# Turning values, keys and outputs by crossbar transfers and GpSimd copies in place of TensorE, from the eighth segment on

## The chip, the cores and the metric

The kernel runs on one core of a Trainium2 chip. A core has a matrix engine (TensorE, rows "PE" for its matmuls and "PEld" for its weight loads), three engines for elementwise work (VectorE "DVE", ScalarE "ACT", GpSimd "POOL"), SyncE ("SP"), which here only starts transfers, and 16 DMA engines that carry them. Each engine works through its own instructions in order and stops at an instruction whose semaphores have not come. The metric is device time in microseconds of one launch. The kernel before takes 2149.38 us, the median of three runs (2148.78 to 2149.49).

## What is computed

One layer of a backbone over 2048 latent tokens of width 1024, with 256 context tokens in front of it. One projection feeds two groups of heads: eight heads of a gated linear recurrence, run forward and backward, and a short convolution. Their outputs go through one output projection. Around the change stands the recurrence:

```
S_t = diag(f_t) S_{t-1} + k_t v_t^T        o_t = S_t^T q_t       (forward and backward, o_f + flip(o_b))
k   = 1 - f          f = lb + (1 - lb) * sigmoid(z)
y   = o * rsqrt(mean(o*o, over the head) + EPS) * onorm_w * silu(gate)
```

Per head k, v, q and o have 128 channels; all of it is float32.

## The kernel before

**Tiling.** The tokens are cut into four groups of 512. A segment is one head on one group: 8 heads x 4 groups = 32 segments. Even heads go through their groups forwards, odd ones backwards. A tile of a segment has channels on the 128 partitions and 512 tokens along the row; its four chunks have 128 tokens each.

**Windows.** The program is written window by window. A window holds the projection of one segment as two or three `units` (one for both gates, one for value and query, in every second window one more for the output gates), and beside them the `chain`, which is the recurrence of the segment before, and `extra` steps: the second direction of the head before, its normalisation and its outputs. A unit consists of seven products (function `seven`, lines 930 to 932) of 12 matmuls each, in a scheme that saves the eighth product of a 2x2 block multiplication. Each step of chain and extra has a weight (`paced(weight, fn)`, table PACE); `merge_steps` lays the steps over the window in proportion to their weights, and `tick`, called after every three matmuls of a product, writes the next step when its share has been reached. So weights decide where among the products' matmuls a step stands in TensorE's order. After the 32 segments come four windows of the convolution, 14 of paired groups, and the output projection.

**The chain of a segment** (`scan_steps`): `value_turn` turns the value tile by four TensorE transposes into PSUM, copied out by ScalarE (lines 555 and 557); five `levels` and `level6` build the in-segment attention from small matmuls on K and Q, while VectorE multiplies K and Q by running products of f (L485, L492); the last matmuls of that are L657, and the last change of K stands behind them. `key_turn` then turns both halves of K, one per direction, into PSUM (L672, eight transposes), ScalarE copies them out (L674); `states` multiplies turned keys with turned values (L681, four matmuls per direction, two instructions each in the profile) and updates the states; `outp` makes the output (L737, L738). For the outputs, `y_steps` scales the output tile (L825), turns it (`turn`, L831), and VectorE multiplies the turned tile, read from PSUM, by the gate (L833).

**Queues.** All loads and stores but 15 of the last stores stand in SP's order. Among them are `hop` loads (L1389): nine buffers of 512 KB hold the operands of the projection, and each load waits until TensorE has read the buffer's old content. Transfers use eight semaphores in turn, so a transfer also waits for the one eight places ahead of it. GpSimd copies Q aside for every second level (`held`, L608) and puts diagonal blocks into the attention tile (L665).

Tiles tagged `pair` are four buffers of 2 KB per partition, used before the change by the operand stores of the early windows and by the scan of the output weights in the last heads.

## Time and profile before

| | |
|---|---|
| median of three runs | 2149.38 us |
| span of the profiled execution | 2150.1 us |
| granted TensorE clock | 0.994 of full speed |
| PE matmuls busy | 2073.2 us, 96% |
| VectorE, ScalarE, GpSimd busy | 77%, 55%, 9% |
| share of the DMA engines' time, main queue | 42.9% |
| first and last turned key tile of a segment | 126.0 to 1265.3 us |

The profiled execution's own time is its span of 2150.1 us, 0.7 us above the median of the runs. A busy TensorE is the union of matmuls whose ends are modelled; the spacing of the starts of successive matmuls says more about what one costs. Rows of groups name line, engine, operation, tiles, shape and count, then busy time, the mean length of one, and idle time before it with what ended it. A number behind "us to landing" counts from the issue to the arrival of the whole transfer.

### The profile page before, as it was taken

What the parts mean: (1) busy time and instruction counts of PE and PEld (TensorE: products, weight loads), DVE (VectorE), ACT (ScalarE), POOL (GpSimd) and SP (SyncE); (2) the same over time, 40 slices, a digit from 0 to 9 for tenths busy, and PEclk for the clock granted to TensorE, in tenths of its full rate; (3) what the DMA queues carried; (4) which work ended last, traced back from release to release, by engine and by line L of the source; (5) the groups of instructions that cost most, each with busy time, mean ns of one, the idle gap of its engine ahead of it and who ended that gap; (6) DMA issues with size and microseconds to landing.
All of it is one profiled execution on the core that took longest, in us unless ns stands there. A gap on an engine that the chain in (4) does not pass through costs nothing.

```text
span 2150.1 us, 53050 instructions
## 1 busy us (share of the span) xinstructions
PE 2073.2 (96%) x22111; PEld 1466.0 (68%) x22111; DVE 1645.8 (77%) x3413; ACT 1192.2 (55%) x2406; POOL 191.8 (9%) x272
## 2 busy tenths in 40 slices
PE   5988999999999999999999999999999999999998
PEld 2877878888888888888888887444444444444443
DVE  6787988878778787788687887678778656687775
ACT  7965666757567666576676654354445423333332
POOL 0121111111111110111110100000000000000000
PEclk9999999999999999999999999999999999999999
DMA  9567533442344233424543458933442105642421
GB/s 356 191 207 265 178 126 134 137 158 72 114 129 146 97 114 109 153 81 142 194 131 127 130 165 260 285 108 110 134 149 93 54 23 196 206 143 92 137 79 59
DMA packets 185798, 311.02 MB, mean 145 GB/s; under 512 B 13010, under 2 KB 114770, under 8 KB 183764
## 3 DMA queue, kind: packets, MB, share of 16 engines
q1 hardware_dynamic: 183396, 303.68, 42.9%
q8 instruction: 173, 2.83, 0.5%
q10 hardware_dynamic: 2160, 3.93, 0.5%
q14 instruction: 69, 0.57, 0.1%
HBM read 240.19 MB, written 67.37 MB: 143 GB/s over the span
## 4 chain that ended last, share of the span: by engine, by line
PE 65%; DVE 18%; ACT 7%; DMA 4%; issue 3%; POOL 1%; SPq 0%; POOLq 0%; ACTq 0%; DVEq 0%
PE sa L930 8%; PE sa L932 8%; PE sa L931 8%; PE sb L930 4%; PE sb L932 4%; PE sb L931 4%; PE sa_o L930 2%; PE sa_o L931 2%; PE sa_o L932 2%; DVE Q L492 2%; PE sc L930 2%; PE sc L931 2%; PE sc L932 2%; DVE K L485 2%; PE T L681 2%
## 5 line engine op out<-in xcount | busy, mean ns | idle before, releaser
L931 PEld LDWEIGHTS <-e_p 128*128 128x128 f16 x1332 | 130.4, 98 | 59.8 <-issue 10.3
L930 PEld LDWEIGHTS <-e_p 128*128 128x128 f16 x1332 | 130.4, 98 | 54.0 <-issue 1.1
L601 ACT ACTIVATE km<-K 128x512 f32<-128x512 f32 x192 | 129.6, 675 | 67.2 <-DVE K L485 61.1
L932 PEld LDWEIGHTS <-e_p 128*128 128x128 f16 x1332 | 130.3, 98 | 51.4
L485 DVE TENSOR_TENSOR K<-K,tot 128x512 f32<-128x512 f32 x192 | 132.2, 689 | 42.9 <-ACT km L601 25.3
L492 DVE TENSOR_TENSOR Q<-Q,tot 128x512 f32<-128x512 f32 x192 | 132.5, 690 | 34.9 <-POOL qm L608 19.5
L608 POOL COPY qm<-Q 128x512 f32<-128x512 f32 x96 | 80.8, 842 | 794.4 <-DVE Q L492 778.7
L931 PEld LDWEIGHTS <-whib_p 128*128 128x128 f16 x888 | 86.9, 98 | 42.1 <-issue 8.8
L930 PEld LDWEIGHTS <-whib_p 128*128 128x128 f16 x888 | 86.8, 98 | 36.7 <-issue 0.8
L930 PEld LDWEIGHTS <-whia_p 128*128 128x128 f16 x888 | 87.0, 98 | 35.7 <-DMA hop3B<-Hd3B 2.3
L932 PEld LDWEIGHTS <-wloa_p 128*128 128x128 f16 x888 | 87.0, 98 | 34.2
L931 PEld LDWEIGHTS <-whia_p 128*128 128x128 f16 x888 | 87.0, 98 | 33.9 <-issue 1.5
L932 PEld LDWEIGHTS <-wlob_p 128*128 128x128 f16 x888 | 86.8, 98 | 34.0
L157 ACT ACTIVATE e_p<-ws_p,sc_p 128x512 f16<-128x512 f32 x108 | 77.5, 718 | 54.9 <-DVE ws_p L444 42.0
L665 POOL COPY A<-Ac 32x128 f32<-32x128 f32 x128 | 77.2, 603 | 128.3 <-ACT A L661 110.6
L853 ACT ACTIVATE cv<-c,small 128x512 f32<-128x512 f32 (+1 forms) x36 | 24.2, 673 | 106.8 <-DVE c L871 61.1
L937 ACT ACTIVATE u<-sa,sx_w 128x256 f32<-128x256 f32 (+1 forms) x111 | 58.1, 524 | 43.5 <-PE sa L932 34.7
L937 ACT ACTIVATE p<-sa,sx_w 128x256 f32<-128x256 f32 (+1 forms) x111 | 57.4, 517 | 39.9 <-PE sa L932 39.8
L158 DVE SCALAR_TENSOR_TENSOR e_p<-ws_p,sc_p,e_p 128x512 f16<-128x512 f32 x108 | 79.4, 750 | 0.0
L409 ACT ACTIVATE junk<-ws_p 128x1024 f16<-128x1024 f32 x72 | 75.7, 1052 | 6.5 <-DMA ws_p<-in_w_in 6.3
L1596 POOL TENSOR_TENSOR x_o<-x_o,fw 128x512 f32<-128x512 f32 x1 | 1.3, 1262 | 868.0 <-ACT junk L1587 868.0
L937 ACT ACTIVATE p<-sb,sx_w 128x256 f32<-128x256 f32 (+1 forms) x111 | 57.8, 521 | 30.8 <-PE sb L932 28.0
(858 smaller groups left out, 7036.3 us busy)
## 6 DMA issues: line engine op xcount, KB each, us to landing
ws_p<-in_w_in SPq DMA_DIRECT2D x72, 512.0 KB, 4.3
y_o<-yT SPq DMA_DIRECT2D x32, 512.0 KB, 4.3
xt_x<-in_x SPq DMA_DIRECT2D x16, 512.0 KB, 6.2
wa<-in_w_ada SPq DMA_DIRECT2D x16, 512.0 KB, 10.2
Gd<-zs SPq DMA_DIRECT2D x32, 256.0 KB, 2.7
sg<-Gd SPq DMA_DIRECT2D x32, 256.0 KB, 4.4
wos<-in_w_out SPq DMA_DIRECT2D x32, 256.0 KB, 5.0
yT<-y SPq DMA_DIRECT2D x32, 256.0 KB, 2.9
```

The source lines that it names most:

```text
L157: S.activation(hi, src, AF.Copy, scale=st[:, 0:1])
L158: V.scalar_tensor_tensor(lo, src, st[:, 0:1], hi, ALU.mult, ALU.subtract)
L409: S.activation(junk.rearrange("p (k n) -> p k n", k=KT), stage[i], AF.Abs, accum_out=r)
L485: V.tensor_tensor(m, m, sub(cur, nb + 1, [[2, np_], [-(nb + 1), 2], [0, B]]), ALU.mult)
L492: V.tensor_tensor(m, m, sub(cur, 1, [[2, np_], [nb - 1, 2], [0, B]]), ALU.mult)
L601: S.activation(sub(s.km, 0, [[2 * B, n // (2 * B)], [B, 2], [1, B]]), mix(s.K, n, B, n // (2 * B)), AF.Copy)
L608: G.tensor_copy(sub(qm, 0, [[2 * B, n // (2 * B)], [B, 2], [1, B]]), mix(s.qf, n, B, n // (2 * B)))
L665: G.tensor_copy(A3[js, :, js], s.Ac[js])
L930: PE.matmul(ps, hi[:, k], rh, start=start and k == 0, stop=False, skip_group_check=not start)
L931: PE.matmul(ps, hi[:, k], right(name, 1, k), start=False, stop=False, skip_group_check=not start)
L932: PE.matmul(ps, lo[:, k], rh, start=False, stop=k == nk - 1, skip_group_check=not start)
L937: last_keep.append(S.activation(r, ps, AF.Copy, scale=sx))
```

## The change

For the 25 segments from the eighth on (head 1's last segment, all of heads 2 to 7), three turns leave TensorE: values, both directions' keys, and outputs (the last not for head 7). A turn becomes three steps (`turn_steps`): `over` sends the tile, read as 128 x 1024 halves of 16 bits, through the DMA crossbar, which puts columns on partitions; `back` gathers the halves of each number with four plain transfers inside SBUF, each of 64 partitions x 4 x 128 halves; `join` lets GpSimd write the two planes of halves interleaved into a ring tile. All transfers are issued by SP, the buffers are of tag `pair`. A turn thus adds one crossbar transfer, four plain ones and one copy; there are 96 turns. Output tiles are multiplied by the gate from SBUF instead of PSUM (`product`). Value turns start ahead of `begin` and end ahead of the third level; the key steps have weights that add to 4.2 where `key_turn` had 1.0.

```diff
+BY_DMA = 7
...
+    def turn_steps(src, make, nm, after=(1.0, 1.0)):
+
+        t = {}
+
+        def over():
+            t["a"] = hp.tile([P, 2 * NCH, P], U16, tag="pair", name=f"ta_{nm}", bufs=4)
+            SY.dma_start_transpose(t["a"], src().bitcast(U16))
+
+        def back():
+            t["b"] = hp.tile([P, NCH, 2, P], U16, tag="pair", name=f"tb_{nm}", bufs=4)
+            for h in range(2):
+                for b in range(2):
+                    SY.dma_start(t["b"][64 * b:64 * b + 64, :, h, :], t["a"][h::2, b::2, :])
+
+        def join():
+            G.tensor_copy(make().bitcast(U16).rearrange("p (c d h) -> p c d h", c=NCH, h=2),
+                          t["b"].rearrange("p c h d -> p c d h"))
+
+        return [paced(after[0], over), paced(after[1], back), paced(0.3, join)]
...
-        return ([paced("values", s.value_turn), paced("begin", s.begin_levels)]
-                + [paced("levels", lambda: s.levels(0)), paced("held", lambda: s.held(1)),
-                   paced("levels", lambda: s.levels(2)), paced("held", lambda: s.held(3)),
+        values = [paced("values", s.value_turn)]
+        held_v = []
+        if s.fast:
+            values, held_v = [], turn_steps(lambda: s.vT, new_value, f"v{s.nm}", (0.2, 0.2))
+        keys = [paced("keys", s.key_turn)]
+        if s.fast:
+            s.kT = []
...
+            two = [turn_steps(lambda i=i: s.K[:, i * s.n:(i + 1) * s.n], lambda i=i: new_keys(i), f"k{s.nm}{i}") for i in range(2)]
+            keys = ([paced(0.0, two[0][0][1]), paced(1.2, two[1][0][1]), paced(0.0, two[0][1][1]), paced(1.2, two[1][1][1]),
+                     paced(0.2, two[0][2][1]), paced(1.6, two[1][2][1])])
+        return (values + held_v[:1] + [paced("begin", s.begin_levels)] + held_v[1:2]
+                + [paced("levels", lambda: s.levels(0)), paced("held", lambda: s.held(1))]
+                + held_v[2:] + [paced("levels", lambda: s.levels(2)), paced("held", lambda: s.held(3)),
                    paced("levels", lambda: s.levels(4))]
-                + [paced("held", lambda: s.held(5)), paced("level6", s.level6), paced("keys", s.key_turn), paced("states", states),
+                + [paced("held", lambda: s.held(5)), paced("level6", s.level6)] + keys + [paced("states", states),
                    paced("out", outp)])
...
+        def product():
+            y = ring(f"y_{s.nm}")
+            V.scalar_tensor_tensor(y, s.oT, onw, s.sg, ALU.mult, ALU.mult)
+            put_y(h.hd, s.tok0 // GW, y)
+
+        end = [paced("turn_y", turn)]
+        if s.fast and h.hd < HEADS - 1:
+            end = turn_steps(lambda: s.o, make, f"o{s.nm}", (0.5, 0.5)) + [paced("turn_y", product)]
...
             s = Seg(hd, g * GW, GW, 0, f"{hd}_{g}")
+            s.fast = hd * NG + i >= BY_DMA
```

How the change moves instructions is seen best at the second segment of head 4, whose chain stands in a window with two units.

SP's order in that window before, from the first operand load of the next segment but one to the load that follows the output (hop: operands, zs and sg: output gates, y: an output tile):

```order
L1389 DMA hop19T_12048<-Hd3T_100 128x2048
L753 DMA yT_113<-y_0_12066 128x512
L818 DMA sg_2_12592<-Gd_108 128x512
L1389 DMA hop19B_12137<-Hd3B_101 128x2048
L1389 DMA hop19T_12153<-Hd3B_99 128x2048
L1389 DMA hop19B_12204<-Hd3B_101 128x2048
```

and now (ta: turned halves, tb: gathered halves; o, k and v name the turn):

```order
L120 DMA_TRANSPOSE ta_o_0_12035<-Q_0_10371 128x8x128
L1444 DMA hop19T_12137<-Hd3T_100 128x2048
L126 DMA tb_o_0_12142<-ta_o_0_12035 64x4x128 x4
L120 DMA_TRANSPOSE ta_k_10_12211<-K_1_11165 128x8x128
L120 DMA_TRANSPOSE ta_k_11_12213<-K_1_11165 128x8x128
L1444 DMA hop19B_12223<-Hd3B_101 128x2048
L126 DMA tb_k_10_12230<-ta_k_10_12211 64x4x128 x4
L126 DMA tb_k_11_12235<-ta_k_11_12213 64x4x128 x4
L1444 DMA hop19T_12249<-Hd3B_99 128x2048
L1444 DMA hop19B_12274<-Hd3B_101 128x2048
L795 DMA yT_113<-y_0_12264 128x512
```

The two crossbar transfers of the keys and their eight plain transfers stand between operand loads; one such load stands between `over` and `back`, and two stand behind the eight.

TensorE's order at the same segment, before, from the key turn to the products of turned keys and values (sc: an accumulator of the projection):

```order
L672 MATMUL kT_10_12161<-ident,K_1_11091 128x128 x4
L672 MATMUL kT_11_12168<-ident,K_1_11091 128x128 x4
...
L932 MATMUL sc_12157<-hop18B_11634,wloa_p_10426 128x256
L681 MATMUL T_10_12184<-v_1_11818,kT_10_12166 128x128 x4
L681 MATMUL T_11_12197<-v_1_11818,kT_11_12173 128x128 x4
```

and now, from the last attention matmuls:

```order
L680 MATMUL A_4_1_12147<-Q_1_11695,K_1_11165 32x64 x16
...
L985 MATMUL sb_12204<-hop18B_11771,e_p_10493 128x256
L986 LDWEIGHTS e_p_10493
L986 MATMUL sb_12204<-hop18B_11771,e_p_10493 128x256
L704 MATMUL T_10_12283<-v_1_11981,kT_10_12257 128x128 x4
L704 MATMUL T_11_12296<-v_1_11981,kT_11_12259 128x128 x4
```

The eight transposes are gone, and between the last attention matmuls and the first product of keys and values now stand 69 matmuls of 128 x 256; before there were 36 and the eight transposes.

GpSimd's order there, before and now:

```order
L608 COPY qm_4_1_12053<-Q_1_11615 128x512
L665 COPY A_1_12112<-Ac_1_11871 32x4x32 x4
L608 COPY qm_4_2_12387<-Q_2_12277 128x512
```

```order
L688 COPY A_1_12183<-Ac_1_11948 32x4x32 x4
L129 COPY oT_0_12221<-tb_o_0_12142 128x1024
L129 COPY kT_10_12257<-tb_k_10_12230 128x1024
L129 COPY kT_11_12259<-tb_k_11_12235 128x1024
L631 COPY qm_4_2_12466<-Q_2_12367 128x512
```

Copies of an output tile and of both key tiles now stand between the diagonal blocks of this segment and the first copy of Q of the next.

More of the change, by code (lines that the diff above doesn't have):

```diff
@@ L13 @@
 I32 = mybir.dt.int32
+U16 = mybir.dt.uint16
 U8 = mybir.dt.uint8
@@ L512, in __init__ @@
             s.small = n < GW
+            s.fast = False
             s.f = s.K = None
@@ L740, in outp, with new_value, new_keys @@
             S.activation(s.o, po, AF.Copy)
-        return ([paced("values", s.value_turn), paced("begin", s.begin_levels)]
-                + [paced("levels", lambda: s.levels(0)), paced("held", lambda: s.held(1)),
-                   paced("levels", lambda: s.levels(2)), paced("held", lambda: s.held(3)),
+        def new_value():
+            s.v = ring(f"v_{s.nm}")
+            return s.v
+        values = [paced("values", s.value_turn)]
[5 more added lines that the diff above has]
+            s.kT = []
+            def new_keys(i):
+                s.kT.append(ring(f"kT_{s.nm}{i}"))
+                return s.kT[i]
+            two = [turn_steps(lambda i=i: s.K[:, i * s.n:(i + 1) * s.n], lambda i=i: new_keys(i), f"k{s.nm}{i}") for i in range(2)]
[4 more added lines that the diff above has]
+                + held_v[2:] + [paced("levels", lambda: s.levels(2)), paced("held", lambda: s.held(3)),
                    paced("levels", lambda: s.levels(4))]
-                + [paced("held", lambda: s.held(5)), paced("level6", s.level6), paced("keys", s.key_turn), paced("states", states),
+                + [paced("held", lambda: s.held(5)), paced("level6", s.level6)] + keys + [paced("states", states),
                    paced("out", outp)])
@@ L834, in turn, with make @@
             put_y(h.hd, s.tok0 // GW, y)
-        return ([paced(0.0, gate)] if own_gate else []) + [paced("scale", scale), paced("turn_y", turn)]
+        def make():
+            s.oT = ring(f"oT_{s.nm}")
+            return s.oT
+        def product():
[5 more added lines that the diff above has]
+            end = turn_steps(lambda: s.o, make, f"o{s.nm}", (0.5, 0.5)) + [paced("turn_y", product)]
+        return ([paced(0.0, gate)] if own_gate else []) + [paced("scale", scale)] + end
     class Conv:
```

## The prediction

> **What bounds the kernel now.** I read the busy times by stretch first, over the stretch in which segments 8 to 32 run their chains:
>
> ```profile
> core 0: us, PE busy (x) PEld busy (x) DVE busy (x) ACT busy (x) POOL busy (x), PEclk, DMA share, GB/s
> 400.00:700.00 300.00, 295.37 (x4446) 261.59 (x4444) 241.04 (x532) 191.38 (x427) 40.09 (x56) 1.00 0.38 123
> 700.00:1000.00 300.00, 295.76 (x4449) 261.94 (x4447) 239.12 (x537) 194.37 (x444) 39.62 (x56) 1.00 0.37 119
> 1000.00:1270.00 270.00, 261.14 (x4134) 231.15 (x4133) 210.72 (x461) 179.61 (x424) 37.66 (x56) 0.99 0.43 139
> ```
>
> TensorE is busy for 852 of 870 us; VectorE has 20% to spare, ScalarE 35%, GpSimd 87%, the DMA engines 60%. The waits of TensorE in that stretch are small:
>
> ```profile
> PE A L631 <- POOL qm L608: 6.1, 7, 2.7
> PE sa L930 <- ACT u L937: 3.0, 10, 0.6
> PE A L631 <- DVE Q L492: 1.9, 7, 0.3
> PE sa L930 <- DVE f L941: 1.7, 5, 0.5
> PE T L681 <- ACT kT L674: 1.6, 3, 0.8
> ```
>
> So each matmul taken away shortens the span by its own length, and each new wait of TensorE lengthens it: the two sides of the sum are counted on this one engine.
>
> **What goes.** 25 segments lose 4 value and 8 key transposes, 21 lose 4 output transposes: 300 + 84 = 384. One costs what it pushes the next weight load back. Loads of the projection follow every 0.11 us; with four transposes between two of them the gap is 0.54:
>
> ```profile
> 705.81 0.10 PEld L932 LDWEIGHTS <-e_p 128*128 128x128 f16 x1
> 705.92 0.47 PEld L672 LDWEIGHTS kT_c<-ident,K_c 128*128 128x128 f32 x4
> 706.35 0.10 PEld L930 LDWEIGHTS <-e_p 128*128 128x128 f16 x1
> ```
>
> Four cost 0.43 us, one 0.108, 384 cost 41.5 us. The busy times of the groups give the upper bound:
>
> ```profile
> L672 PE MATMUL kT<-ident,K 128*128 128x128 f32 x256 | 34.3, 274 | 1.0 <-DVE Q L777 1.0
> L831 PE MATMUL oT<-ident,Q 128*128 128x128 f32 x128 | 20.1, 277 | 0.7 <-ACT Q L825 0.5
> L555 PE MATMUL vt<-ident,vT 128*128 128x128 f32 x128 | 19.8, 278 | 0.4 <-DVE s_c L704 0.4
> ```
>
> 200 x 34.3/256 + 84 x 20.1/128 + 100 x 19.8/128 = 55.5 us, but that counts tails of matmuls under which the next one runs. I take 41.5. Also 75 copies of ScalarE go (0.59 us each, 44 us); with 35% idle on ScalarE and TensorE waiting for it for a few us, I cost that gain at nothing. VectorE's product of the outputs reads SBUF instead of PSUM, one instruction for one.
>
> **What comes, and what hides it.** 480 more transfers on SP, 0.32 us to start each, as all starts there (row below): 154 us on a queue that mostly waits. 96 copies on GpSimd. Neither engine is near its end. What can reach TensorE is time from one end to the other: a key turn is crossbar, then gathering, then the copy, one behind the other, and TensorE stops at the product of keys and values (line 681 before) until the copy is there. Values have far more room (their first reader is the same product, but they start at the window's begin), outputs too (their steps are spread over a window).
>
> The time from the last change of K to turned keys. The last attention matmuls end at 610.33 (609.70 + 0.63), VectorE's last product on K 0.75 us later:
>
> ```profile
> 609.70 0.63 PE L657 MATMUL A<-Q,K 128*32 128x64 f32 x32
> 610.39 0.69 DVE L485 TENSOR_TENSOR K<-K,tot 128x512 f32<-128x512 f32 x1 [0.24 <-PE A L657]
> ...
> 614.96 0.27 PE L932 MATMUL sc<-hop14B,wloa_p 128*128 128x256 f16 x1
> 615.07 1.97 PE L681 MATMUL T<-v,kT 128*128 128x128 f32 x16
> 616.88 0.27 PE L930 MATMUL sa<-hop14T,e_p 128*128 128x256 f16 x1
> ```
>
> Then the transfers, bounded by these:
>
> ```profile
> 735.57 0.32 SPq L1389 DMA_DIRECT2D hop18T<-Hd2T  x1
> ...
> yT<-y SPq DMA_DIRECT2D x32, 256.0 KB, 2.9
> yT<-sg SPq DMA_DIRECT2D x64, 128.0 KB, 2.4
> out<-x_o SPq DMA_DIRECT2D x17, 256.0 KB, 2.1
> xt_x<-in_x SPq DMA_DIRECT2D x16, 512.0 KB, 6.2
> wa<-in_w_ada SPq DMA_DIRECT2D x16, 512.0 KB, 10.2
> ```
>
> No crossbar transfer is in the trace. It moves 256 KB out of SBUF; the nearest row is the output tile's store, same size, same source: X = 2.9 us. Bounds: 2.1 (the fastest row of 256 KB) and 10.2 (the slowest landing of the list). The gathering: four starts of 0.32, 1.3 us, and 2.4 for the last of them (64 KB; the smallest row is 128 KB). The copy on GpSimd handles 1024 halves; the rows are of 512 elements:
>
> ```profile
> L608 POOL COPY qm<-Q 128x512 f32<-128x512 f32 x96 | 80.8, 842 | 794.4 <-DVE Q L492 778.7 <-DMA hb_x<-Xd 15.6
> L301 POOL TENSOR_SCALAR hop<-h_x 128x512 f16<-128x512 f32 x8 | 6.2, 782 | 10.3 <-ACT h_x L296 9.7 <-ACT h_x L292 0.5
> ```
>
> Half the bytes written change little, so the count of elements sets it: 1.7 us, not the 0.84 that equal bytes would give. Sum for the first key tile: 0.75 + 2.9 + 1.3 + 2.4 + 1.7 = 9.0 us after the attention matmuls; the second follows on GpSimd at 10.7.
>
> The time that TensorE has. It is filled with the matmuls that stand between. Before, 36 matmuls of 128 x 256 and eight transposes: 36 x 0.11 + 8 x 0.108 = 4.8 us, and the trace has 615.07 - 610.33 = 4.74. Now 69 at this place: 7.6 us. Counted in the same way over the 25 segments: 7.6 us at seven of them (the second segment of heads 2 to 7, and head 7's last); 8.9 and 10.1 at the first segments of even and odd heads, three each; 9.5 to 14 at the other twelve. Even heads multiply the first tile first and need the second 0.9 us later (half of 1.81, from 615.07 to 616.88); odd heads begin with the second.
>
> Waits: at 7.6, even (heads 2, 4, 6): 1.4, and then the second tile, needed at 9.9 and there at 10.7, 0.8: 3 x 2.2 = 6.6. At 7.6, odd or last (four): 3.1 each, 12.4. First segments: 3 x 0.1 and 3 x 0.6, 2.1. The other twelve: none. In sum 21.1 us.
>
> One more piece at the seven: the eighth gathering transfer reuses the semaphore of the operand load between `over` and `back`. That load leaves when a product 2.3 us behind the attention matmuls (21 matmuls) has ended, and lands some 4.3 us later:
>
> ```profile
> hop11B<-Hd3B SPq DMA_DIRECT2D x3, 512.0 KB, 4.3
> ```
>
> So at 6.6 in place of 0.75 + 2.9 + 7 x 0.32 = 5.9: 0.7 us, 7 x 0.7 = 4.9.
>
> What queues behind. While SP waits for a crossbar transfer, operand loads wait behind it, some 2.4 us by the terms above. From the release of a buffer to its next reader stand at least 11.5 us of matmuls in the new order in this stretch, and the slowest operand load lands in 7.3 us:
>
> ```profile
> hop3T<-Hd3T SPq DMA_DIRECT2D x3, 512.0 KB, 7.3
> ```
>
> That leaves 1.8 us: hidden, but a crossbar transfer of 5 us would use it up.
>
> **Sum.** 41.5 - 21.1 - 4.9 = 15.5 us. The profiled execution takes 2150.1 us, so 2134.6; the median of the runs lies 0.7 us lower, so 2134 for the time, 0.7% faster. Its own range, from X between 2.3 and 3.6 (13 us per us of X, since the seven and the six all wait) and a copy between 0.84 and 1.7: 2118 to 2144.
>
> **Rivals.**
>
> Everything hidden (2113). With X at 2.1 and 0.84 us per copy, tiles are there at 7.4 and 8.3: only the odd ones of the seven wait, 4 x 0.7, and a little at their semaphore, 5 us with all. 2149.4 - 41.5 + 5. For it: DMA engines 60% free, GpSimd 87%. Against it: both low ends at once.
>
> The gain is eaten (2145 to 2154, which is within 0.2%, about what a measurement of this kernel tells from no change). X from 3.7 to 4.4: 15.5 us divided by 13 is 1.2, so at X = 4.1 the new waits equal the transposes.
>
> Key tiles late: slower (2166). One mechanism at one place: the crossbar transfer lands later than a plain one of its size, and TensorE stands at the key product in most segments. It decides from X = 4.4. Loads of 256 KB land later than stores:
>
> ```profile
> ha_x<-Xd SPq DMA_DIRECT2D x8, 256.0 KB, 5.1
> ```
>
> At 5.1, the thirteen places wait 2.2 us more each, 28.6, and the twelve others begin (some 4): 2134 + 33 = 2167, so about 2166; at 6.2, when the twelve wait 0.8 us each, 2187. For it: two changes of layout in a row on a queue that also carries 512 KB loads, and a pattern finer than any in the trace. Against it: DMA engines 60% idle.
>
> Block by block (2280). If the eight blocks of 128 x 128 halves went through one after another, X would be at the far bound, 10.2: 7.3 us more at thirteen places, 95, and some 4 us more at each of the others, 50. The Trainium skill, page "VectorE: DVE Perf Modes", section "The three transpose paths", has such a rule: 1309 ns for a 128 x 128 block of 16 bits by crossbar against 390 ns by TensorE, and TensorE wherever PSUM will do; eight in a row are 10.5 us, an estimate. No run so far shows a crossbar transfer, so nothing of this trace agrees or disagrees; what speaks against eight in a row is that twice the bytes (128 to 256 KB) make a plain transfer only 0.5 us longer (2.4 to 2.9).
>
> **Chances.** My forecast 0.40, everything hidden 0.11, eaten 0.14, late 0.29, block by block 0.06. Faster by over 0.2%: 0.51; within: 0.14; slower: 0.35. The range takes 2112 to 2188: from everything hidden to X = 6.2, leaving out some 0.15.
>
> **What would show it.** Transposes 384 fewer, the matmuls otherwise the same, so about 41 us less PE busy time. In the waits, TensorE's at the product of keys and values, for GpSimd's copy: about 26 us, 2 to 4 us at the second segment of each head, nothing at the third and fourth. The crossbar transfer from issue to landing: 2.9 us; the gathering 2.4; GpSimd's copy 1.7. Wrong would be: waits of TensorE for operand loads (SP held too long), for copies of Q (GpSimd held by a copy that waits for its transfer), or a crossbar transfer that also holds SP much longer than 0.32 us.

## The result, and the profile after

The changed kernel takes 2307.6 us (median of four runs, 2304.1 to 2308.8) against 2149.2 us before: a ratio of 1.073, with a 95% interval of 1.0719 to 1.0745. It is 158 us slower; the forecast was 15 us faster. The profiled execution spans 2302.4 us against 2150.1.

The stretches that were read before, in the changed kernel (columns as before: length, then busy time and instructions of TensorE, its weight loads, VectorE, ScalarE and GpSimd, the granted clock, the DMA engines' share and GB/s):

```profile
400.00:700.00 300.00, 259.49 (x3884) 226.62 (x3882) 216.34 (x458) 152.40 (x348) 64.71 (x77) 0.94 0.57 147
700.00:1000.00 300.00, 259.27 (x3752) 224.60 (x3749) 214.29 (x450) 153.95 (x355) 65.77 (x76) 0.94 0.64 157
1000.00:1270.00 270.00, 228.93 (x3192) 197.91 (x3179) 193.51 (x406) 152.72 (x341) 58.05 (x67) 0.91 0.63 162
```

TensorE, busy for 98% of this time before, is now busy for 86%, and its granted clock is 0.91 to 0.94 where it was 1.00. No other engine is near its end: VectorE falls from 80% to 72%, GpSimd stands at 22%, and the DMA engines go from 0.38 to 0.6. So nothing is full, and TensorE waits all the same. The part that was 915 us long (355 to 1270) is now 1067 (355 to 1422); TensorE's gaps in it (idle times over 50 ns), added up from its instructions, are 156.5 us against 18.1. The stages behind it have kept their times.

What it waits for, and who else waits, in rows taken from the list of waits (total us, times, longest):

```profile
POOL kT L129 <- DMA tb_k<-ta_k: 213.1, 44, 12.8
POOL v L129 <- DMA tb_v<-ta_v: 119.6, 19, 17.5
DVE S L748 <- PE T L704: 90.6, 21, 12.3
PE T L704 <- POOL kT L129: 78.4, 24, 8.8
POOL oT L129 <- DMA tb_o<-ta_o: 40.8, 12, 6.4
DVE y L884 <- POOL oT L129: 19.6, 7, 4.5
PE A L654 <- POOL qm L631: 13.9, 8, 5.6
PE sa L984 <- DVE z L995: 13.2, 6, 4.6
```

The wait that the forecast spoke of, TensorE at the product of keys and values (T, now line 704) for GpSimd's copy, is there: 78.4 us in place of 26, in 24 waits at 22 of the 25 segments. The other half of the 156 us of gaps stands at lines for which the forecast's sum had nothing. VectorE ends 55 us of them, most at line 984, where an accumulator is not yet evacuated; copies of Q by GpSimd end 16 us (6 before). VectorE itself waits in order: its update of the state (line 748) for the late product, its product of the outputs (line 884) for the turned output.

The second segment of head 3 (heads counted from 0), one of the seven places with the least room, is in the forecast's own terms (timeline: start, length, engine and line; in brackets the idle time before and what ended it):

```profile
635.39 0.63 PE L680 MATMUL A<-Q,K 128*32 128x64 f32 x32
650.31 3.78 PE L704 MATMUL T<-v,kT 128*128 128x128 f32 x16 [5.66 <-POOL kT L129]
...
636.09 0.69 DVE L507 TENSOR_TENSOR K<-K,tot 128x512 f32<-128x512 f32 x1 [0.49 <-PE A L680]
652.43 0.35 DVE L748 SCALAR_TENSOR_TENSOR S<-S,tot,T 128x128 f32<-128x128 f32 x1 [6.35 <-PE T L704]
...
636.55 1.22 SPq L126 DMA_DIRECT2D tb_o<-ta_o  x1
637.87 2.81 SPq L120 DMA_TRANSPOSE ta_k<-K  x2
640.77 0.99 SPq L1444 DMA_DIRECT2D hop15B<-Hd0B  x1
642.14 5.26 SPq L126 DMA_DIRECT2D tb_k<-ta_k  x8
...
646.84 1.14 POOL L129 COPY kT<-tb_k 128x1024 uint16<-128x1024 uint16 x1 [4.55 <-DMA tb_k<-ta_k]
649.11 1.15 POOL L129 COPY kT<-tb_k 128x1024 uint16<-128x1024 uint16 x1 [1.13 <-DMA tb_k<-ta_k]
```

The attention matmuls end at 636.02 and K is final at 636.78, 0.76 us later, as forecast. SP starts the crossbar transfers 1.1 us after that, since it is still starting an output's gathering. The two starts hold it for 2.8 us, the eight gathering starts for 5.3. The tiles are there at 647.98 and 650.26, 12.0 and 14.2 us behind the attention matmuls, where 9.0 and 10.7 were forecast; this head multiplies the second one first, and TensorE stands 5.66 us, not 3.1; over the 25 segments the means are 13.7 and 16.5.

What a start costs SP, and when a transfer lands (the view of the tile ta_k: shortest, median and longest time at SP in ns, first and last start; the third row is the landing of the crossbar transfers; behind it the gatherings' size and landing from the list of transfers):

```profile
L120 SPq DMA_TRANSPOSE ta_k<-K x50: 1231/1264/2291, 390.1 to 1407.2; - x50
L126 SPq DMA_DIRECT2D tb_k<-ta_k x200: 593/616/1546, 395.2 to 1415.5; - x100
DMA to landing us min/median/max: 2.2/3.1/8.7
```

```profile
tb_k<-ta_k SPq DMA_DIRECT2D x200, 64.0 KB, 2.5
```

The crossbar transfer lands after 3.1 us (forecast 2.9), a gathering after 2.5 (2.4), and GpSimd's copy takes 1.15 (1.7). What was mis-sized is the start: 1.26 and 0.62 us in place of 0.32. The trace before already had starts on SP longer than 0.32 us, such as these stores of weights (view of the tile WdT):

```profile
L1035 SPq DMA_DIRECT2D WdT<-wpT x32: 513/517/1280, 1383.1 to 1663.9; - x32
```

### The profile page after: what moved, and what is told of

The parts are those of the page before. It is cut to its first block, busy times and chain, and to the rows that moved or that the text cites. A ratio compares the mean times of both kernels' runs of the same rounds, so it can differ in the third digit from the quotient of the medians.

```text
span 2302.4 us, 53148 instructions
## 1 busy us (share of the span) xinstructions
PE 2088.9 (91%) x21727; PEld 1465.3 (64%) x21727; DVE 1687.8 (73%) x3413; ACT 1162.8 (51%) x2331; POOL 299.8 (13%) x368
## 4 chain that ended last, share of the span: by engine, by line
PE 53%; DVE 21%; DMA 12%; SPq 4%; ACT 4%; issue 3%; POOL 3%; POOLq 0%; DVEq 0%; ACTq 0%
PE sa L984 6%; PE sa L985 6%; PE sa L986 6%; SPq L126 3%; DVE Q L514 3%; PE sb L984 3%; PE sb L986 3%; PE sb L985 3%; DMA tb_k<-ta_k 3%; PE T L704 2%; PE sa_o L984 2%; PE sa_o L986 2%; PE sa_o L985 2%; DVE K L507 2%; DMA ta_k<-K 1%
## 5 line engine op out<-in xcount | busy, mean ns | idle before, releaser
L507 DVE TENSOR_TENSOR K<-K,tot 128x512 f32<-128x512 f32 x192 | 139.4, 726 | 46.1 <-ACT km L624 30.4
L704 PE MATMUL T<-v,kT 128*128 128x128 f32 x512 | 95.1, 354 | 80.9 <-POOL kT L129 78.4
L514 DVE TENSOR_TENSOR Q<-Q,tot 128x512 f32<-128x512 f32 x192 | 139.2, 725 | 29.3 <-POOL qm L631 15.3
L704 PEld LDWEIGHTS T<-v,kT 128*128 128x128 f32 x512 | 86.3, 259 | 105.0 <-POOL kT L129 91.7
L748 DVE SCALAR_TENSOR_TENSOR S<-S,tot,T 128x128 f32<-128x128 f32 x120 | 41.0, 342 | 89.1 <-PE T L704 88.0
L129 POOL COPY kT<-tb_k 128x1024 uint16<-128x1024 uint16 x50 | 61.2, 1227 | 213.4 <-DMA tb_k<-ta_k 213.1
L688 POOL COPY A<-Ac 32x128 f32<-32x128 f32 x128 | 68.7, 537 | 101.5 <-ACT A L684 86.2
## 6 DMA issues: line engine op xcount, KB each, us to landing
wa<-in_w_ada SPq DMA_DIRECT2D x16, 512.0 KB, 10.2
```

The lines of the kernel that those rows point to most:

```text
L507: V.tensor_tensor(m, m, sub(cur, nb + 1, [[2, np_], [-(nb + 1), 2], [0, B]]), ALU.mult)
L514: V.tensor_tensor(m, m, sub(cur, 1, [[2, np_], [nb - 1, 2], [0, B]]), ALU.mult)
L688: G.tensor_copy(A3[js, :, js], s.Ac[js])
L704: PE.matmul(pt[:, sl], s.kT[i][:, sl], s.v[:, sl], start=True, stop=True)
```

## The experiments

All are built from the changed kernel. "Gaps" are TensorE's idle times over 50 ns, added up from 355 us to the last product of keys and values (1256 to 1661 us, by kernel). "VectorE held" is worked out in the same stretch: for each group of VectorE's instructions (one line, operation and tile), what an instruction took beyond the shortest of its group, where that is over 0.2 us. Some groups mix sizes, which makes some 6 to 9 us of the number in every kernel; counted by size as well, it is 0 before and 48 in the change. "Half clock" is the time of the whole run in which the granted clock is 0.5. All three are in us.

| Kernel | Time | Ratio to before | Gaps | VectorE held | Half clock |
|---|---|---|---|---|---|
| before | 2149.2 | 1 | 18 | 6 | 27 |
| the change | 2307.6 | 1.073 | 156 | 55 | 171 |
| keys on TensorE (e1) | 2185.9 | 1.016 | 59 | 37 | 50 |
| only keys by crossbar (e2) | 2273.6 | 1.058 | 117 | 32 | 114 |
| larger weights for the key turn (e3) | 2301.5 | 1.071 | 154 | 52 | 120 |
| four whole-row transfers (e4) | 2300.4 | 1.070 | 152 | 59 | 144 |
| plain transfer for the crossbar's (e6) | 2269.4 | 1.056 | 126 | 52 | 142 |
| halves apart first, slow walk (e7) | 2539.2 | 1.181 | 346 | 410 | 380 |
| the same, keys on TensorE (e8) | 2319.6 | 1.079 | 154 | 198 | 142 |
| two whole-row transfers (e9) | 2299.4 | 1.070 | 140 | 50 | 158 |
| halves apart first, in order (e10) | 2248.6 | 1.046 | 114 | 122 | 82 |
| only values by crossbar (e11) | 2149.0 | 1.000 | 25 | 28 | 21 |
| the change, copies on ScalarE (e12) | 2279.0 | 1.060 | 136 | 11 | 134 |
| keys from a ready tile (e13) | 2239.8 | 1.042 | 108 | 72 | 98 |
| only values, copies on ScalarE (e14) | 2139.0 | 0.995 | 18 | 11 | 19 |
| values and outputs, ScalarE (e15) | 2173.5 | 1.011 | 51 | 10 | 28 |
| waits filled, 16 products (e16) | 2313.2 | 1.076 | 93 | 47 | 92 |
| ready tile, copies on ScalarE (e17) | 2194.0 | 1.021 | 78 | 9 | 53 |
| waits filled, 8 products (e18) | 2302.9 | 1.071 | 118 | 55 | 102 |

### Which of the three turns costs (e1, e2)

```diff
         keys = [paced("keys", s.key_turn)]
-        if s.fast:
+        if False:                                   # e1
...
-        if s.fast:
+        if False:                                   # e2, for values, and the same for outputs
             values, held_v = [], turn_steps(...)
```

> The keys of all segments are turned on TensorE again; values and outputs still go by crossbar. Theory (the key turn is too long for the room behind the attention matmuls, above all because each start of a gathering holds SP 0.62 us and not 0.32): what is left has room, so only the 184 saved transposes count, 184 x 0.108 = 20 us: 2130 to 2142 us, and the stretches of half clock go back to about those of before (27 us). Rival (the values' and outputs' turns cost as well: GpSimd's copies wait in order for their transfers, SP is held): over 2155, with TensorE waiting for copies of Q and for evacuations by VectorE.

> Only the keys go by crossbar; values and outputs are turned on TensorE. Theory: most of the loss stays, though SP has half as many starts, since the key turn alone still holds SP 2 x 1.26 + 8 x 0.62 = 7.5 us in a row: 2220 to 2290 us. Rival (values and outputs crowd SP and GpSimd, and the keys are late only because of them): 2125 to 2160.

The keys cost most: alone they make 2273.6, as the theory said. But values and outputs are not free. With keys on TensorE the time is 2185.9 [ratio 1.0145 to 1.0182], 38 us above before (2148.2 in the same runs) where 20 us less were expected, so e1's rival came out and its theory did not. The two losses, 125 and 38 us, add up to 163, close to the change's 158. In e1 ScalarE ends 32 of the 59 us of gaps and VectorE 18. One place, from the timeline of e1 (VectorE, then ScalarE, then TensorE):

```profile
642.64 0.75 DVE L884 SCALAR_TENSOR_TENSOR y<-oT,small,sg 128x512 f32<-128x512 f32 x1 [5.07 <-POOL oT L129]
...
644.75 1.15 ACT L179 ACTIVATE whia_p<-ws_p,sc_p 128x1024 f16<-128x1024 f32 x1 [5.43 <-DVE sc_p L174]
645.80 0.46 ACT L991 ACTIVATE u<-sa,sx_w 128x256 f32<-128x256 f32 x1
...
646.31 0.37 PE L984 MATMUL sa<-hop15T,e_p 128*128 128x256 f16 x1 [6.08 <-ACT u L991]
```

VectorE stands 5.07 us at the product of a turned output. Behind it on VectorE are the scales of a weight tile (sc_p), for which ScalarE waits; behind that on ScalarE is the evacuation u, for which TensorE stands 6.08 us. So an output that is late by a few us reaches TensorE through what is queued behind its product.

### More room, fewer pieces, fewer starts (e3, e4, e9)

```diff
-... paced(1.2, two[1][0][1]), ..., paced(1.2, two[1][1][1]), ..., paced(1.6, two[1][2][1])
+... paced(3.6, two[1][0][1]), ..., paced(3.6, two[1][1][1]), ..., paced(4.8, two[1][2][1])   # e3
...
-            for h in range(2):
-                for b in range(2):
-                    SY.dma_start(t["b"][64 * b:64 * b + 64, :, h, :], t["a"][h::2, b::2, :])
+            for q in range(4):                                                     # e4
+                SY.dma_start(t["b"][32 * q:32 * q + 32]..., t["a"][1 + 64 * (q % 2):64 + 64 * (q % 2):2])
+            for q in range(2):                                                     # e9
+                SY.dma_start(t["b"][64 * q:64 * q + 64]..., t["a"][1::2])
```

> The steps of the key turn are given three times the share of the window, so that more matmuls of the projection stand between the last attention matmul and the product of keys and values; nothing else is changed, and the same transfers are issued. Theory: the waits of TensorE at that product (170 us by the list of waits, 80 us of idle TensorE) fall below 40, and the halved clock and the late evacuations go with them: 2150 to 2215 us. Rival (the transfers themselves, by their small pieces and the DMA engines' time, or the held operand loads, slow the whole stretch): still over 2260.

> The four transfers behind each crossbar transfer copy whole rows of 2 KB (32 pieces each) in place of 256 pieces of 256 bytes; as many starts, as many bytes. Left out: the gathering, so keys, values and outputs are not the reference's. Theory: a start costs SP by its pieces, so it falls from 0.64 us to 0.32 or less, a key tile comes some 2.5 us earlier (8 x 0.32), TensorE's waits at the key product are halved, and the time falls by 40 to 110 us, to 2200 to 2265. Rival 1 (a start behind a crossbar transfer costs 0.64 whatever its pieces): over 2290 and the start unchanged. Rival 2 (the crossbar transfer's own latency decides): the start falls, but the time stays over 2285.

> Two transfers of 64 whole rows (128 KB each) stand in place of the four gathering transfers behind each crossbar transfer; the bytes are the same. Left out: the gathering, so the outputs are not the reference's. A start behind a crossbar transfer kept its 0.6 us when its pieces went from 256 to 32. Theory (the number of starts, one behind the other on SP, is what makes the key tiles late): the first tile comes 1.2 us earlier and the second 2.4 us, at 25 places where TensorE stands some 3 us each: 30 to 60 us less, 2245 to 2280. Rival (SP's starts matter little; the crossbar transfer, GpSimd's copies and what waits behind them decide): over 2290.

All three expectations of the theory missed. In e3 the product comes 15.8 us behind the attention matmuls on average, against 15.5: a window's matmuls are shared out among its steps, so what the keys got the attention levels lost, and TensorE's gaps there for copies of Q rose from 11 to 30 us. In e4 a start still takes 0.59 us with 32 pieces in place of 256, so its price is not the number of pieces. In e9 half the starts saved SP its time, but the larger transfers landed later (the group of the copies that wait for them, then the list of transfers; 64 KB above, 128 KB here):

```profile
L128 POOL COPY kT<-tb_k 128x1024 uint16<-128x1024 uint16 x50 | 62.6, 1264 | 217.9 <-DMA tb_k<-ta_k 215.6
```

```profile
tb_k<-ta_k SPq DMA_DIRECT2D x100, 128.0 KB, 4.5
```

4.5 us in place of 2.5: the tiles came 0.7 and 1.2 us earlier, not 1.2 and 2.4, TensorE's waits at the product did not fall (91.6 us), and the time fell by 8 us. The intervals of all three ratios overlap the change's, so none of these gains is clear of the noise. The theory that SP's starts alone make the loss fell here.

### The crossbar's part (e6)

```diff
-            SY.dma_start_transpose(t["a"], src().bitcast(U16))
+            SY.dma_start(t["a"], src().bitcast(U16).rearrange("p (b c) -> p b c", b=2 * NCH))
...
-            G.tensor_copy(make().bitcast(U16)..., t["b"]...)
+            G.tensor_copy(make().bitcast(U16)...("p (n h) -> p n h", h=2), sub(t["b"], 1, [[2, GW], [0, 2]]))
```

> A plain transfer of the same 256 KB stands in the crossbar transfer's place; the gathering and the copies stay. Left out: the turn itself, so the outputs are not the reference's (GpSimd's copy takes 512 halves twice each, so that all numbers are finite). Theory (gathering starts are the larger part): SP saves 2 x 1.0 us at a key turn and the landing some 0.5 us: the time falls by 40 to 80 us, less than with whole rows in the gathering, and stays over 2225. Rival 2 (the crossbar transfer is the cause): under 2190.

A plain transfer at the crossbar's place takes 38 us off, just short of the 40 to 80 expected: its start holds SP 0.5 us in place of 1.3. Three quarters of the loss stay, so the crossbar transfer itself is not the main cause.

### Halves apart first: no gathering, but a copy more on GpSimd (e7, e8, e10)

```diff
+        def split():
+            t["b"] = hp.tile([P, 2, GW], U16, ...)
+            G.tensor_copy(t["b"].rearrange("p h n -> p n h"), src()...("p (n h) -> p n h", h=2))   # e7, e8
+            G.tensor_copy(t["b"], src()...("p (n h) -> p h n", h=2))                               # e10
         def over():
-            SY.dma_start_transpose(t["a"], src().bitcast(U16))
+            SY.dma_start_transpose(t["a"], flat(t["b"]))
-        def back():
-            ... four gathering transfers ...
         def join():
-            G.tensor_copy(..., t["b"].rearrange("p c h d -> p c d h"))
+            G.tensor_copy(..., t["a"].rearrange("p (h c) d -> p c d h", h=2))
...
+            if s.fast:                     # in level6, behind the last change of K
+                s.split()
...
+            keys = [paced(0.0, two[0][1][1]), paced(2.4, two[1][1][1]), paced(0.2, two[0][2][1]), paced(1.6, two[1][2][1])]
```

> The order of the three parts is changed: GpSimd first copies low and high halves apart, then one crossbar transfer turns both planes, then GpSimd's second copy joins the halves; the four gathering transfers go. All turned tensors are the reference's. Theory: per key turn SP is left with two starts of 1.3 us in place of 2 x 1.3 + 8 x 0.64, and the first tile comes at 0.75 + 1.2 + 1.3 + 3.1 + 1.2 = 7.5 us, the second at 8.8, against 13.7 and 16.5: TensorE's waits at the key product fall under 25 us, and the time comes to 2110 to 2160. Rival (in-order waits of GpSimd's copies and of SP for crossbar transfers cost by themselves): over 2190, with TensorE waiting for copies of Q or evacuations.

> As the run with the halves copied apart first, but the keys stay on TensorE; values and outputs go by crossbar. Theory: the gatherings' starts, 184 x 0.64 us, are what made values and outputs late on SP and VectorE; without them the 184 transposes are saved for nothing: 2125 to 2145 us, under the kernel before. Rival (copies that wait in order on GpSimd hold the copies of Q, and VectorE's product of the outputs holds VectorE): over 2155.

> Halves copied apart first, as before, but the copy walks one plane after the other (it writes 512 halves in a row) instead of alternating between the planes, which took 5.0 us a copy. All turned tensors are the reference's. Theory: the copy takes 1.2 us; key tiles come at 7.5 and 8.8 us, no gathering starts are left, TensorE's waits at the key product fall under 25 us; what stays is VectorE, which is held while GpSimd copies (55 us over its own time in the changed kernel, 402 us with the copies of 5.0 us), now some 80 to 110 us: 2180 to 2270. Rival 1 (gatherings and key tiles explain everything): under 2150. Rival 2 (in-order waits for crossbar transfers explain it): over 2290.

e7 and e8 became the dearest kernels of all; e8's 2319.6 lies with its rival (over 2155), but for a reason that neither expectation had. GpSimd's copy that writes the two planes in turn takes 5.1 us, not 1.2, and VectorE's products on K become longer with it (groups of e7; then, from its timeline, GpSimd's two copies and a VectorE instruction beside each):

```profile
L120 POOL COPY tb_k<-K 128x1024 uint16<-128x1024 uint16 x50 | 246.0, 5130 | 29.7 <-DVE K L505 28.8
L505 DVE TENSOR_TENSOR K<-K,tot 128x512 f32<-128x512 f32 x192 | 202.0, 1052 | 34.8 <-ACT km L622 20.0
```

```profile
645.75 10.79 POOL L120 COPY tb_k<-K 128x1024 uint16<-128x1024 uint16 x2
...
646.53 4.30 DVE L518 TENSOR_TENSOR tot<-tot 128x256 f32<-128x256 f32 x1
651.89 4.55 DVE L505 TENSOR_TENSOR K<-K,tot 128x512 f32<-128x512 f32 x1
```

An instruction of 0.69 us takes 4.55, until GpSimd's copy is done. In the changed kernel the same is there on a smaller scale (GpSimd, then VectorE):

```profile
695.39 1.14 POOL L129 COPY oT<-tb_o 128x1024 uint16<-128x1024 uint16 x1
...
695.47 1.61 DVE L514 TENSOR_TENSOR Q<-Q,tot 128x512 f32<-128x512 f32 x1 [0.31 <-POOL qm L631]
```

The same instruction takes 0.69 us elsewhere. Of the 48 us that the change's VectorE is held by size, all lie beside an instruction of GpSimd, 44 beside a joining copy. The Trainium skill, page "SBUF — State Buffer", section "Who interferes with whom", has this as a rule: a VectorE instruction with two inputs in SBUF and a GpSimd instruction that reads SBUF wait for each other, whichever starts later. These rows, in which GpSimd started first, agree.

e10 mends the walk. The copy takes 1.03 us at its shortest, the waits at the key product fall to 35.0 us (under 25 were expected), and the time to 2248.6, inside the theory's range, with VectorE held for 122 us:

```profile
L704 PE MATMUL T<-v,kT 128*128 128x128 f32 x512 | 82.5, 321 | 40.9 <-POOL kT L127 35.0
```

### Keys that are always ready, and copies on ScalarE (e12, e13, e17)

```diff
-... turn_steps(lambda i=i: s.K[:, i * s.n:(i + 1) * s.n], ...)
+... turn_steps(lambda i=i: hc[:, 0, 0].rearrange("p k t -> p (k t)"), ...)          # e13, e17
...
-            G.tensor_copy(make().bitcast(U16)..., t["b"]...)
+            S.activation(make().bitcast(U16)..., t["b"]..., AF.Copy)                # e12, e17
```

> The change as it is, with the joining copies on ScalarE in place of GpSimd. Theory A (GpSimd's 16-bit copies keep VectorE from its second operand, and that is a large part): VectorE's time over its own falls from 55 to about 10 us, and the time to under 2260. Theory B (engines that wait in order for the transfers are what costs): ScalarE now carries the waits of GpSimd for gatherings (370 us by the list of waits) and its evacuations come late: over 2330.

> The key turns read a resident operand tile of the same size in place of K: the same transfers, starts and copies at the same places in every engine's order, but they need not wait for K. Left out: the turning of the keys, so the outputs are not the reference's. Theory A (the key tiles are late: the parts of the turn one behind the other after K's last change): TensorE's waits at the key product fall from 80 us to under 15, what waits behind them and most of the halved clock go too: 2160 to 2195, near the run with keys on TensorE (2186) less 200 transposes (21.6). Theory B (load: DMA engines, SP and GpSimd's copies are busier): over 2230.

> As the run whose key turns read a tile that is always ready (2240), with all joining copies on ScalarE in place of GpSimd; left out again: the turning of the keys. Theory A (GpSimd's copies keep VectorE from its second operand): VectorE's time over its own falls from 72 to about 10 us, and the time by 30 us or more, under 2210. Theory B (DMA engines and SP, busy with the transfers, make the rest): within 15 us of 2240, or more, since ScalarE now waits in order for the transfers.

These three divide the loss. With a source that is always ready, the same transfers and copies cost 68 us less (2239.8): that is what the lateness of the key tiles is worth, with all that waits behind it, though 19.5 us of waits at the key product are left. It is less than half of the loss, so e13's theory B is the nearer one. With the copies of that kernel on ScalarE, the time falls by another 46 us (2194.0), and VectorE is held for 9 us in place of 72: both numbers of e17's theory A. The gaps of TensorE that VectorE ends fall with it, from 54 to 21 us. The other way in which GpSimd could have cost this, copies of Q that stand behind a waiting joining copy, is not it: TensorE's gaps for them do not fall (11 and 14 us in the segments' stretch; the rows below are of line 654, whole run). Without the ready source the same move takes 28 us: in e12 VectorE is held for 11 us, as its theory A said, but the time is over its 2260. ScalarE there ends 97 of 136 us of gaps, 68 of them at the key product, as it waits in order for the late transfers. TensorE's waits at the key product and for copies of Q in e13, the same in e17, and VectorE's products on K in e17 (689 ns each before):

```profile
PE T L704 <- POOL kT L129: 19.5, 8, 4.4
...
PE A L654 <- POOL qm L631: 9.2, 13, 1.4
```

```profile
PE A L654 <- POOL qm L631: 16.1, 12, 2.4
PE T L704 <- ACT kT L129: 12.9, 11, 3.3
```

```profile
L507 DVE TENSOR_TENSOR K<-K,tot 128x512 f32<-128x512 f32 x192 | 133.0, 693 | 61.9 <-ACT km L624 41.7
```

### What the halved clock costs (e16, e18)

After most of TensorE's longer gaps the granted clock is halved. In the changed kernel each of 23 stretches of half clock in the segments' part begins within 5 us after the start of a gap, and their lengths are 3.4, 6.8, 10.2 or 13.7 us; one gap of 2.57 us and seven of 1.5 to 1.9 are followed by none. Two of them show in the timeline and the windows (columns as above); the second gap is 2.03 us:

```profile
949.53 0.37 PE L984 MATMUL sa<-hop22B,whia_p 128*128 128x256 f16 x1 [4.49 <-DVE z L995]
949.69 3.69 PE L704 MATMUL T<-v,kT 128*128 128x128 f32 x16
...
777.19 1.48 PE L704 MATMUL T<-v,kT 128*128 128x128 f32 x8 [2.03 <-POOL kT L129]
```

```profile
777.90:784.50 6.60, 6.37 (x102) 5.52 (x101) 4.90 (x14) 4.54 (x15) 1.14 (x1) 0.74 0.94 310
```

The 16 recorded matmuls of a key product take 3.69 us at half clock where they took 1.97 before. The Trainium skill, page "TensorE: Matmul & The Clock Gate", section "Part 1: The HAM clock gate (the "warmup" mystery)", lets the clock fall after an idle window of about 3.4 us. This trace does not agree at eleven of the 23 places: the longest gap ahead of the halved stretch was 2.0 to 2.9 us at eight and 1.4 to 1.9 at three.

```diff
             pt = px_t(f"T_{s.nm}{i}")
+            if s.fast and len(s.Ss) == 0:
+                for _ in range(4):                                                 # e16; 2 in e18
+                    for ch in range(s.n // P):
+                        sl = slice(ch * P, (ch + 1) * P)
+                        PE.matmul(pt[:, sl], s.v[:, sl], s.v[:, sl], start=True, stop=True)
...
+            s.Ss = []
             pp = s.outer(prim)
-            s.Ss = []
```

> The change as it is, with 16 matmuls (128 x 128, some 1.8 us) ahead of each of the 25 first key products, into the same PSUM tile, where the product overwrites them; they need no key tile. Theory (gaps of some 2 us and more are followed by stretches of half the clock, some 55 us in all): the gap that is left is mostly under 2 us, stretches of half clock in this part fall by a third or more, and the time falls by 8 to 30 us, though 45 us of matmuls were added. Rival (the clock matters little): the time rises by 5 to 25 us, as matmuls are added where the wait was shorter than 1.8 us.

> The change as it is, with 8 products (some 1.75 us at full clock) ahead of each of the 25 first key products, half of the fill that was tried before (2313). 44 us of matmuls are added. Theory (halved clock behind the gaps is worth 40 us or more): the gap at these places falls under 2 us, the halved stretches fall from 171 us to about 120, and the time falls by 8 us or more, under 2300. Rival (the halved clock is worth little, since TensorE waits for other engines there anyway): 2303 to 2320.

Both theories missed the time, though the half clock fell as e16's said and further than e18's. The rivals' times came out: a rise of 6 us, and 2302.9, at the lower end of 2303 to 2320. The fill of e16 was twice what I wrote: eight products take 1.81 us (the prediction's row at 615.07), so 16 take 3.6 us, longer than most gaps. In e18 the fill is 25 x 1.81 = 45 us, the gaps fall by 39, and the time falls by 5 (its interval, 1.0686 to 1.0725, and the change's, 1.0719 to 1.0745, overlap a little); in e16 it is 90, 63 and a rise of 6. What is left for the clock is 45 - 39 + 5 = 11 us for 69 us less at half clock, and 90 - 63 - 6 = 21 us for 79 less. By these shares, and if the fill changed nothing else, the 144 us that the change added at half clock cost some 23 to 38 us, an estimate: part of the loss, but not its body.

### Values alone, and outputs (e11, e14, e15)

```diff
+        if False:                          # keys (e11, e14, e15) and outputs (e11, e14): turned on TensorE
-            G.tensor_copy(...)
+            S.activation(..., AF.Copy)     # e14, e15
-                + held_v[2:] + [paced("levels", lambda: s.levels(2)), paced("held", lambda: s.held(3)),
-                   paced("levels", lambda: s.levels(4))]
+                + [paced("levels", lambda: s.levels(2)), paced("held", lambda: s.held(3))] + held_v[2:]   # e14, e15
+                + [paced("levels", lambda: s.levels(4))]
-            end = turn_steps(lambda: s.o, make, f"o{s.nm}", (0.5, 0.5)) + [paced("turn_y", product)]
+            end = turn_steps(lambda: s.o, make, f"o{s.nm}", (0.5, 2.0), 2.0) + [paced("turn_y", product)]   # e15
```

> Only the values go by crossbar; keys and outputs are turned on TensorE. Against the run with values and outputs (2186) it tells which of the two costs. Theory: VectorE's product of the outputs waits in order for the turned output (up to 5 us) and holds weights and evacuations behind it, 19 us of TensorE's waits; without it, and with 84 transposes (9 us) back: 2160 to 2175. Rival (the values' copies hold GpSimd's copies of Q, and these cost): over 2180. Rival (values cost nothing): 2149 - 100 x 0.108 = 2138.

> Only the values go by crossbar, and their joining copies are on ScalarE, two pairs of levels later. With GpSimd's copies the values gave no gain (2149.0 against 2149.3) and VectorE was held 28 us over its own time, 6.5 before. Theory (VectorE held by GpSimd's copies, and GpSimd's copies of Q behind a waiting copy, ate the gain): 25 x 1.17 us on ScalarE are hidden, VectorE's excess goes under 10 us, and the 100 transposes are saved: 2138 to 2144. Rival (what was gained is lost on ScalarE, whose evacuations come later): 2147 or more.

> Values as in the run before, and outputs by crossbar too, with copies on ScalarE and more room between transfer, copy and product (weights 2.0 and 2.0 in place of 0.5 and 0.3). With copies on GpSimd and little room the outputs cost 37 us. Theory (VectorE's product waited in order for the turned output): 184 transposes saved, 2129 to 2142. Rival (the outputs' four gatherings each on SP hold operand loads and other stores): over 2150, with TensorE's waits for operands or evacuations.

Values alone with copies on GpSimd give 2149.0, no gain at all (ratio 0.9987 to 1.0009); that is 11 us below the range of e11's theory and above the 2138 of its rival. With copies on ScalarE, behind one more pair of steps (`levels(2)`, `held(3)`), they give 2139.0 against 2150.8 in the same runs: a ratio of 0.995 (0.9937 to 0.9963), or 10.7 us (8 to 14), in the range of e14's theory. The 100 transposes by the forecast's price are 10.8 us. So this version beats both kernels. Engine and place of the copy changed together, so the 10 us between e11 and e14 are not divided between them; TensorE's gaps for VectorE fell from 11 to 5 us and those for copies of Q from 4 to 1. A stretch of e14, and the group of its copies:

```profile
400.00:700.00 300.00, 296.23 (x4455) 262.44 (x4454) 247.61 (x547) 197.02 (x430) 41.03 (x56) 1.00 0.48 140
```

```profile
L129 ACT ACTIVATE v<-tb_v 128x1024 uint16<-128x1024 uint16 x25 | 29.2, 1169 | 14.4 <-DMA tb_v<-ta_v 14.4
```

98.7% busy, full clock; ScalarE has room for 29 us of copies and waits 14 us for them in all. With outputs as well (e15) the time is 2173.5, still 1.1% above before, in spite of four to seven times the weight between the steps: 84 transposes, worth 9 us, cost 34 net; e15's rival had the number. TensorE then waits mostly for ScalarE (40 of 51 us of gaps, most at lines 984, 704 and 1546). ScalarE waits 21 us in order at the copies of the outputs for their gatherings; whether that is what holds it was not tested.

## Why the prediction was wrong, by its own steps

**What bounds the kernel: right.** TensorE sets the time. e14 shows it best: 100 transposes less, and the time is shorter by their length.

**What goes: right.** 0.108 us a transpose held where it could be measured: 10.8 us expected, 10.7 (8 to 14) in e14; that the two agree to a tenth is luck. For the other 284 transposes no run shows the gain alone, so the whole 41.5 us are an estimate by this price.

**The key turn: mechanism and place right, and most of its terms.** K final at 0.75, the crossbar's 2.9 us (3.1) and the gathering's 2.4 (2.5) were right within 0.2 us, and the copy's 1.7 was too high (1.15, between its bounds). The step that failed here is "480 more transfers on SP, 0.32 us to start each, as all starts there": the row was of a load from DRAM, the same trace had starts of 0.5 us and more, and a crossbar start takes 1.26 us, a gathering start 0.62. In the turn's sum this stood as 1.3 us of gathering; SP needs 2.8 us for two crossbar starts and 5.3 for eight gatherings, and is late itself, since other turns' gatherings stand ahead. The waits at the product are 78.4 us, not 26, and they stand at the third and fourth segments of heads 2 to 6 too (0.9 to 3.7 us), where none were forecast. But the runs also showed that shorter or fewer starts alone do not bring them back (e4, e9), as what two larger transfers save is lost in later landings; without the gathering (e10) the waits are 35.0.

**What hides it: the sentence that failed most.** "What can reach TensorE is time from one end to the other" left out what is not a latency. Most of the waits at the product, their halved clock and what stands behind them are 68 us by e13. By e17 another 46 are GpSimd's joining copies, through VectorE as far as the waits tell, costed at nothing because neither engine is near its end: a copy does not need VectorE's time, it stops VectorE. And "outputs too" have far more room was true of the output and false of VectorE, which waits in order at its product with weights and evacuations behind it (e1: 5.07 us there become 6.08 on TensorE). Counted from the 2107.7 us that the transposes alone would give by that price (2149.2 - 41.5), the loss is 200 us: 68 by lateness, 46 by VectorE held with the keys ready, and 86 that stay in e17. In those lie the outputs (43 us by e14 and e15: 34 net and their 9), and the rest was not divided. The parts overlap and depend on what else is there (28 us in place of 46 in e12), so they are sizes, not a sum to the microsecond.

**The clock: left out.** The trace before showed it at one place of the segments' stretch, a wait for a copy of Q with half the clock behind it (timeline, then the window):

```profile
1039.02 0.46 PE L631 MATMUL A<-qm,km 128*32 128x32 f32 x32 [2.66 <-POOL qm L608]
```

```profile
1039.40:1042.90 3.50, 3.23 (x56) 2.34 (x46) 2.45 (x6) 2.84 (x10) 0.61 (x1) 0.51 0.70 220
```

The forecast put waits of 2 to 4 us on TensorE and nothing on the clock behind them; by e16 and e18 that is some 23 to 38 us, within the parts above.

**The rivals.** "Key tiles late: slower" had the sign and the place, but its condition (a crossbar transfer of 4.4 us or more) never came: the transfer took 3.1. "Block by block" is refuted by the same row, eight blocks land in 3.1 us and not in 10.2, though the measured time lies beyond its 2280. The Trainium skill, page "VectorE: DVE Perf Modes", section "The three transpose paths", prices a single block at 1309 ns; eight times that was the prediction's own estimate, and eight blocks here take a third of it. The Trainium skill's advice on the same page, section "Rules for kernel authors", is TensorE where PSUM will do: the keys and outputs here agree, the values of e14 do not. "Everything hidden" exists only for the values, and on ScalarE (e14).

**What would show it.** Of the signs named, TensorE's 384 transposes fewer came out, and nearly so the crossbar's and the gathering's landing. TensorE's busy time did not fall by 41 us but rose from 2073 to 2089, as matmuls at half clock take longer. Of the signs of being wrong, "a crossbar transfer that also holds SP much longer than 0.32 us" and waits "for copies of Q" both came; TensorE waited for no operand load in the segments' stretch. The range ended at 2188, with every case in it priced at one place, the key product; none held a cost on a second engine.

## What to carry to other kernels

An engine that is 80% idle can still cost time: ask which engine it stops while it works and what stands in order behind each new wait, not only whether its busy time fits. As these runs suggest, move a turn off the bounding engine only where its first reader comes long after and where the copy that finishes it runs on an engine that holds no other one up: here the values, with copies on ScalarE, gained just the length of their transposes, while keys and outputs lost several times theirs.

## What was not expected of the hardware

- GpSimd's copy of 1024 halves takes 1.15 us reading two planes and writing in a row, and 5.1 us where the writes go to two planes in turn; 1.03 at its shortest where the reads step and the writes don't (e10, median 1.44).
- VectorE instructions with two SBUF inputs wait out a GpSimd copy that started first: 0.69 us becomes 1.61 beside a copy of 1.14, and 4.55 beside one of 5.1.
- A start on SP takes 1.26 us for the crossbar transfer of 128 x 1024 halves and 0.5 to 0.6 us for transfers from SBUF to SBUF, with 32 pieces or 256, where loads from DRAM mostly take 0.32 to 0.42.
- The granted clock is halved for 3.4 us or multiples of it behind 23 gaps of TensorE, of which eleven were under 3 us; other gaps of 1.5 to 2.6 us had no such stretch behind them.
